# Attention's order in a two-layer trunk: gates and compression directly behind the keys, the values' products and the second queries beside the first group's scores

## The chip, the cores and the metric

The kernel runs on one core of a Trainium2 chip. Its engines are TensorE (PE in the profile; its weight loads are shown apart as PEld), VectorE (DVE), ScalarE (ACT), GpSimd (POOL) and SyncE (SP), which issues the transfers. The metric is device microseconds of one execution, all on this one core. The kernel before took 737.44 us (median of 3 runs: 737.44, 735.28 and 738.83).

## The reference, cut to what matters

x is 256 positions by 1024 features, all in float32. There are two layers: a gated linear recurrence and a ConvFFN, then native sparse attention and a ConvFFN, each behind an RMSNorm with shift, scale and gate from a conditioning vector, and a last RMSNorm. The change is in the attention:

```python
q, k_c, v_c, k_s, v_s, k_w, v_w, gate = jnp.split(h @ w_in, split_at, axis=-1)   # 1024, 6 x 256, 48
gate = jax.nn.sigmoid(gate.astype(jnp.float32)).reshape(B, S, G, HPG, 3)
kc = compress(k_c, cmp_pe[0], cmp_w1[0], cmp_w2[0])      # silu(blocks @ w1) @ w2, 15 blocks of 32 positions
vc = compress(v_c, cmp_pe[1], cmp_w1[1], cmp_w2[1])
...
p_c = jax.nn.softmax(jnp.where(valid_c, s_c, NEG_INF), axis=-1)      # s_*: scaled q.k less slope x distance
...
return gb[..., 0, None] * o_c + gb[..., 1, None] * o_s + gb[..., 2, None] * o_w
...
return o.astype(h.dtype) @ w_out
```

G = 4 groups of keys and values serve HPG = 4 heads of 64 features each. With 256 positions all four blocks of 64 positions are selected and the window of 512 covers everything, so the second and third branch are causal attention over all positions with two sets of keys and values.

## The kernel before, in words

The features lie on the partitions: XT is [128, 8 chunks, 256 positions]. The weights are float32 and stream through the kernel once, in units of 512 KB (128x1024). A unit is loaded by SP (L91) into one of 7 raw buffers, cast by ScalarE to a high part `whi` (L104), and VectorE subtracts that from the unit for the low part `wlo` (L107); there are 5 pairs of split buffers. Each float32 product is done as three products of such parts: high x high (L311), high weight x low activations (L312), low weight x high activations (L313). Loading runs up to 7 units ahead of the unit in use and splitting up to 3 ahead. Some units are rows of the conditioning's weights (`ada`), which VectorE sums in the raw buffer (L239), without TensorE.

TensorE and SP run in the order in which the program is written. The order of VectorE and ScalarE is made by a scheduler, with priorities given in the program (`soon`, `high_priority`); inside the attention loop GpSimd is in written order too. The names of PSUM buffers are "mm" and "aux" with two banks each and "acc" with four, and a bank is given out again when its last reader is done.

The attention part is written in this order (the numbers of functions and lines are those of the listing below):

- the products for the keys and the compressed branch's inputs, on eight accumulators, then the copies KV of the compression's inputs (L882) and the high and low parts KH and KL of the keys (L886 to L888);
- the values' products `some_values` (48 products of 128x512 into two "mm" banks), five of the eight chunks ahead of the compression and three behind it, with a loop of early splits between (NSA_SPLIT);
- the compression `hps` (32 matmuls), its offset `pec` (L912) and Silu (L915);
- the gates `gps` (24 products) and their sigmoid `gsb` (L930);
- the first queries, `gen_q(0)`: two units of weights, 48 products 128x256; the compressed keys and values (`kps`, L962, L964) lie between the first unit and the second. At its end ScalarE scales a head into the high half of the tile `QS` (L953) and VectorE forms its low half (L954), head after head, four heads;
- the gates' transposes (L982), and the first half of the second queries `gen_q(1)`;
- the loop over the four groups. `weave` runs generators side by side, always the one that is furthest behind by a weight in us. The first is `scores`: for each pair of heads (k = 0, 1) three pieces; in a piece each head has two score products into an "acc" bank (L1014, L1015), VectorE adds the distances and takes the least (L1019), ScalarE takes the exponential (L1023), VectorE forms the compressed scores `SC` (L1026). After the last piece of a pair of heads `scale` multiplies the probabilities PR by gate over sum: for the first 128 query positions (t = 0) on VectorE, tiles of 128x128 (L1042), for the others (t = 1) on GpSimd, tiles of 128x256 (L1044). Beside a group's scores stand the next group's queries and, from the second group on, `gen_values` of the group before: transposes of PR (L1092, L1096), their copies `pt` (L1102), the products with the values (L1116, L1119) and the high and low parts AH and AL of the result (L1125, L1129).

```python
sides.append((gen_q(g + 1) if g else queries, SIDE))
...
weave((heads, SCORES[g]), *sides)
```

Of the kernel before, what the change touches and what calls it, by code (L numbers as in the profile page):

```python
# [11 lines left out]
FT = mybir.dt.float32  # L12
FR = mybir.dt.float32r
U32 = mybir.dt.uint32
AF = mybir.ActivationFunctionType
# [4 lines left out]
P = 128  # L20
D = 1024
NC = 8
S = 256
# [16 lines left out]
HG_LATE = 6  # L40
FFN_LATE = 8
NSA_ROWS = (11, 3)
NSA_SPLIT = 2
PRE = 2
HG_WEAVE = (16.4, 15.5)
HG_TURN = 14
# [2 lines left out]
SIDE, VALUES = 5.6, 9.5  # L49
# [4 lines left out]
QBLOCK = 4  # L54
# [112 lines left out]
def one_after_another(*gens):  # L167
    for g in gens:
        yield from g
# [3 lines left out]
def trunk(ctx: ExitStack, tc: tile.TileContext, I, out):  # L173
    nc = tc.nc
# [7 lines left out]
    def bank(tag):  # L182
        return psum.tile([P, 512], FT, name=tag, bufs=4 if tag == "acc" else 2)

    def soon():

        return tc.high_priority(offset=SOON)
# [38 lines left out]
    XH = consts.tile([P, NC, S], FR, name="XH")  # L226
    XL = consts.tile([P, NC, S], FR, name="XL")
# [6 lines left out]
    st = Stream(nc, raws, splits, *LOOK)  # L234
# [24 lines left out]
    flat = lambda a: a.rearrange("p a b -> p (a b)")  # L259
    pairs = lambda a: [flat(a[:, k:k + 2]) for k in range(0, NC, 2)]  # L260
# [31 lines left out]
        return ids[:NC], get  # L292

    u_f = [ffn_units(0, ada_units(0, "g2") + ada_units(1, "1") + ada_units(1, "g1"))]
    ws = chunks(I["nsa_a"]) + pairs(I["nsa_v"]) + [flat(I["nsa_gate"])] + chunks(I["nsa_q"]) + chunks(I["nsa_out"])
    rows = ada_units(1, "2")
    a, b = NSA_ROWS
    ids = mix(ws[:12], rows[:a])
    for r in rows[a:a + b]:
        ada(r)  # L300
    ids += mix(ws[12:21], []) + mix(ws[21:], rows[a + b:])
    u_na, u_nv, u_ng, u_nq, u_no = ids[:8], ids[8:12], ids[12], ids[13:21], ids[21:29]
    u_f.append(ffn_units(1, ada_units(1, "g2")))

    for h in range(4):
# [4 lines left out]
    def mm3(o, wh, wl, xh, xl, start, stop):  # L310
        nc.tensor.matmul(o, wh, xh, start=start, stop=False, skip_group_check=True)  # L311
        nc.tensor.matmul(o, wh, xl, start=False, stop=False, skip_group_check=True)  # L312
        nc.tensor.matmul(o, wl, xh, start=False, stop=stop, skip_group_check=True)  # L313
# [174 lines left out]
    def token_major(ps, c, hi, lo, w):  # L488

        for t in range(2):  # L490
            x = slice(t * P, (t + 1) * P)
            mm3(ps[t], XH[:, c, x], XL[:, c, x], hi[:, w], lo[:, w], c == 0, c == NC - 1)
            yield 0.65
# [232 lines left out]
    def run(g):  # L726
        for _ in g:
            pass
# [165 lines left out]
        keys(g, slice(P, S), s[:, :P])  # L894
        keys(g, slice(272, 528), half(acc, 6 + g // 2)[b:b + 64])

    vps = [bank("mm") for _ in range(2)]

    def some_values(c0, c1):
        for c in range(c0, c1):  # L900
            hi, lo = st.use(u_nv[c // 2])
            run(token_major(vps, c, hi, lo, slice((c % 2) * 512, (c % 2 + 1) * 512)))

    some_values(0, 5)
    while st.done < u_ng + NSA_SPLIT:
        st.split()

    hps = bank("aux")
    for l in range(32):
# [4 lines left out]
    with soon():  # L914
        nc.scalar.activation(hid, hps[:, :60], AF.Silu, bias=pec)  # L915

    some_values(5, NC)

    for t in range(2):
        (nc.scalar.copy, nc.vector.tensor_copy)[t](VT[:, t].rearrange("p g d -> p (g d)"), vps[t])  # L920


    gps = bank("aux")
    hi, lo = st.use(u_ng)
    for c in range(NC):
        w = slice(c * P, (c + 1) * P)
        mm3(gps[:, :S], hi[:, w], lo[:, w], XH[:, c], XL[:, c], c == 0, c == NC - 1)
    gsb = big.tile([48, S], FT, name="gsb")
    with soon():
        nc.scalar.activation(gsb, gps[:48, :S], AF.Sigmoid)  # L930

    QS, PR = {}, {}

    def gen_q(g):


        ps = bank("mm")
        for k in range(2):
            for c in range(NC):
                hi, lo = st.use(u_nq[2 * g + k])  # L940
                w = slice(c * P, (c + 1) * P)
                mm3(ps[:, k * S:(k + 1) * S], hi[:, w], lo[:, w], XH[:, c], XL[:, c], k == 0 and c == 0, c == NC - 1)
                if c % QBLOCK == QBLOCK - 1:
                    yield 0.35 * QBLOCK
        QS[g] = att.tile([P, HPG, S], FR, name="QS")
        rest = []
        with tc.high_priority(offset=QSOON[g]):
            for k in range(2):
                for b in range(2):
                    src = ps[64 * b:64 * b + 64, k * S:(k + 1) * S]  # L950
                    h = 2 * k + b
                    f = -HD ** -0.5 / slopes[HPG * g + h]
                    nc.scalar.activation(QS[g][:64, h], src, AF.Copy, scale=f)  # L953
                    nc.vector.scalar_tensor_tensor(QS[g][64:, h], src, f, QS[g][:64, h].bitcast(FT),  # L954
                                                   op0=OP.mult, op1=OP.subtract)
        yield 0.01
# [29 lines left out]
    for t in range(2):  # L986
        nc.vector.tensor_scalar(gate[:, t, 0::3], gate[:, t, 0::3], rowok[:, t:t + 1], None, op0=OP.mult)

    queries = gen_q(1)
    for _ in range(NC // QBLOCK):  # L990
        next(queries)

    BANKS = [[(P, 400, [(0, 0, P, 0, 0), (1, 144, P, P, 0)], P)],
# [3 lines left out]
    def scores(g, k):  # L999
# [31 lines left out]
        def scale():  # L1031
            r = work.tile([P, 2, 2, 2], FT, name="rsum", bufs=3)
            nc.vector.reciprocal(r, ssum)
            for b in range(2):
                nc.vector.tensor_mul(r[:, b], r[:, b], gate[:, :, 3 * heads[b] + 1:3 * heads[b] + 3])
            for b in range(2):
                for t in range(2):
                    for _, _, parts, _ in BANKS[t]:
                        for br, f, n, o, d in parts:
                            p = PR[g][t][:, 2 * k + b, o:o + n]  # L1040
                            if t == 0:
                                nc.vector.tensor_scalar(p, p, r[:, b, t, br:br + 1], None, op0=OP.mult)  # L1042
                            else:
                                nc.gpsimd.tensor_scalar(p, p, r[:, b, t, br:br + 1], 0.0, op0=OP.mult, op1=OP.add)  # L1044
# [102 lines left out]
    with tc.manual_schedule(engines={ET.Pool}):  # L1147
        st.lazy = True
        for g in range(G):
            heads = one_after_another(*[scores(g, k) for k in range(2)])  # L1150
            sides = []
            if g + 1 < G:
                sides.append((gen_q(g + 1) if g else queries, SIDE))
                if g > 0:
                    sides.append((after(BEHIND[0], gen_values(g - 1)), BEHIND[0] + VALUES))
                for _ in range(HEAD[g]):
                    next(heads)
            else:

                acc_o = [bank("acc") for _ in range(4)]  # L1160
                outs = [out_chunk(acc_o, u_no[j], AH[:, j], AL[:, j], j == 0, 4) for j in range(6)]
                next(heads)
                run(outs[0])
                sides.append((after(BEHIND[1], gen_values(g - 1)), BEHIND[1] + VALUES))
                sides.append((one_after_another(*outs[1:BESIDE]), 2.64 * (BESIDE - 1)))
            weave((heads, SCORES[g]), *sides)
        gate_cols(2)
        weave((gen_values(3), VALUES), (one_after_another(*outs[BESIDE:6]), 2.64 * (6 - BESIDE)))
        st.flush()
        st.lazy = False  # L1170
# [97 lines left out]
```

## Time and profile before

| | |
|---|---|
| time, 3 runs | 737.44 us median (735.28 to 738.83) |
| the profiled execution's own time | 740.72 us |
| its span | 738.9 us |
| granted TensorE clock, mean | 0.976 |
| busy share: PE, DVE, ACT, POOL | 95%, 77%, 52%, 14% |
| HBM over the span | 216 GB/s |

The span goes from the first to the last instruction of the profiled execution. Busy time is that of an engine's instructions; time in which an engine waits is not in it. A row of a timeline gives the start, the duration, engine and line, operation, output and inputs, shapes, and in brackets how long the engine sat idle before it and what ended that. Products run in a pipeline: two neighbours start 0.12 us apart though each takes 0.28. The clock is given as a share of the higher of its two levels, 2.4 GHz; 0.5 is the lower, 1.2 GHz.

### The profile page before, as it was taken

To read this page: it belongs to the slowest core of one execution; us is meant where nothing else is said; L and a number is where in the kernel's file an instruction comes from. 1 tells how busy PE (TensorE), PEld (TensorE's weight loads), DVE (VectorE), ACT (ScalarE), POOL (GpSimd) and SP (SyncE) were. 2 spreads that over 40 slices of the span, in tenths; PEclk is the share of its full clock that TensorE was granted. 3 is DMA by queue.
4 is the path that set the end of the run, shared out by engine and by line. 5 is a ranking of instruction groups with operands and counts; after the bars stand their busy time and mean duration, and the time that the engine had idled before them with its cause. 6 is when DMAs were issued, how large, how long until landed. Compare 5 with 4: busy or idle time off the path is not lost.

```text
span 738.9 us, 14320 instructions
## 1 busy us (share of the span) xinstructions
PE 700.9 (95%) x5532; PEld 665.3 (90%) x5532; DVE 572.4 (77%) x1115; ACT 382.1 (52%) x706; POOL 106.3 (14%) x150
## 2 busy tenths in 40 slices
PE   8999899899999999999999997889999999999996
PEld 7878888788999999999999896767899999999995
DVE  5999999998898777789879778986477866666653
ACT  5337444154655444555444667764355555445544
POOL 2000001012012182101130002222110110100112
PEclk8999999999999999999999998999999999999997
DMA  8898757578488888999939951321237676767601
GB/s 315 295 333 314 254 155 251 167 252 290 166 309 286 273 281 279 282 306 339 328 111 321 342 173 33 112 79 40 83 122 250 218 216 198 216 210 221 206 2 57
DMA packets 48854, 160.45 MB, mean 217 GB/s; under 512 B 9361, under 2 KB 9617, under 8 KB 48786
## 3 DMA queue, kind: packets, MB, share of 16 engines
q1 hardware_dynamic: 48496, 159.02, 65.7%
q8 instruction: 43, 0.70, 0.4%
q10 hardware_dynamic: 290, 0.53, 0.2%
q14 instruction: 25, 0.20, 0.1%
HBM read 158.48 MB, written 1.05 MB: 216 GB/s over the span
## 4 chain that ended last, share of the span: by engine, by line
PE 69%; DVE 15%; DMA 5%; issue 4%; ACT 4%; POOL 2%; POOLq 0%; DVEq 0%; ACTq 0%; SPq 0%
PE mm L311 10%; PE mm L313 10%; PE acc L374 10%; PE mm L312 10%; PE acc L313 6%; PE acc L312 6%; PE acc L311 6%; DVE wlo L107 5%; DMA raw<-ada 4%; DVE raw L239 4%; PE aux L597 2%; DMA raw<-hg_out 2%; POOL sq L347 1%; PE aux L1096 1%; PE mm L1119 1%
## 5 line engine op out<-in xcount | busy, mean ns | idle before, releaser
L107 DVE TENSOR_TENSOR wlo<-raw,whi 128x1024 fp32r<-128x1024 f32 x201 | 247.7, 1238 | 69.5 <-ACT whi L104 69.4
L104 ACT CAST whi<-raw 128x1024 fp32r<-128x1024 f32 x201 | 208.0, 1048 | 147.6 <-PE mm L312 45.9
L311 PE MATMUL mm<-XH,whi 128*128 128x256 f32 x672 | 189.6, 282 | 2.0 <-DVE AL L1129 1.1
L313 PE MATMUL mm<-XH,wlo 128*128 128x256 f32 x672 | 188.6, 281 | 0.4 <-DVE wlo L107 0.4
L312 PE MATMUL mm<-XL,whi 128*128 128x256 f32 x672 | 188.2, 280 | 0.0
L239 DVE SCALAR_TENSOR_TENSOR raw<-raw,cb 128x1024 f32<-128x1024 f32 x96 | 119.0, 1242 | 23.5 <-DMA raw<-ada 23.4
L311 PEld LDWEIGHTS mm<-XH,whi 128*128 128x128 f32 x672 | 127.0, 189 | 3.1 <-DVE ff L792 1.5
L313 PEld LDWEIGHTS mm<-XH,wlo 128*128 128x128 f32 x672 | 127.1, 189 | 0.7 <-DVE wlo L107 0.6
L312 PEld LDWEIGHTS mm<-XL,whi 128*128 128x128 f32 x672 | 127.1, 189 | 0.0
L312 PE MATMUL acc<-fl,whi 128*128 128x256 f32 x352 | 98.6, 280 | 0.3 <-POOL fl L797 0.3
L311 PE MATMUL acc<-fh,whi 128*128 128x256 f32 x352 | 98.5, 280 | 0.0
L313 PE MATMUL acc<-fh,wlo 128*128 128x256 f32 x352 | 98.5, 280 | 0.0
L797 POOL TENSOR_TENSOR fl<-ff,fh 128x256 fp32r<-128x256 f32 x44 | 42.8, 977 | 302.5 <-ACT fh L795 294.9
L312 PEld LDWEIGHTS acc<-fl,whi 128*128 128x128 f32 x352 | 66.2, 188 | 0.5 <-POOL fl L797 0.5
L313 PEld LDWEIGHTS acc<-fh,wlo 128*128 128x128 f32 x352 | 66.2, 188 | 0.0
L311 PEld LDWEIGHTS acc<-fh,whi 128*128 128x128 f32 x352 | 66.1, 188 | 0.0
L790 ACT ACTIVATE cv<-cv 128x256 f32<-128x256 f32 x44 | 18.0, 415 | 46.5 <-DVE cv L789 46.3
L374 PE MATMUL acc<-XH,whi 128*128 128x256 f32 x256 | 37.9, 292 | 3.8 <-ACT XH L393 3.8
L374 PEld LDWEIGHTS acc<-XH,whi 128*128 128x128 f32 x256 | 33.9, 196 | 7.1 <-ACT XH L393 7.0
L393 ACT ACTIVATE XH<-xn,sh_t 128x256 fp32r<-128x256 f32 x32 | 15.2, 503 | 41.6 <-DVE xn L392 41.6
L795 ACT CAST fh<-ff 128x256 fp32r<-128x256 f32 x44 | 17.5, 405 | 35.5 <-DVE ff L792 35.4
L374 PE MATMUL acc<-XL,whi 128*128 128x256 f32 x256 | 35.3, 279 | 0.0
(230 smaller groups left out, 1218.6 us busy)
## 6 DMA issues: line engine op xcount, KB each, us to landing
raw<-ada SPq DMA_DIRECT2D x96, 512.0 KB, 4.8
raw<-up SPq DMA_DIRECT2D x88, 512.0 KB, 4.6
raw<-down SPq DMA_DIRECT2D x44, 512.0 KB, 4.6
raw<-hg_a SPq DMA_DIRECT2D x16, 512.0 KB, 5.2
raw<-hg_b SPq DMA_DIRECT2D x8, 512.0 KB, 5.0
raw<-hg_out SPq DMA_DIRECT2D x8, 512.0 KB, 4.5
raw<-nsa_a SPq DMA_DIRECT2D x8, 512.0 KB, 4.8
raw<-nsa_q SPq DMA_DIRECT2D x8, 512.0 KB, 5.4
```

The costliest lines, as they stand in the source:

```text
L104: self.nc.scalar.copy(hi, t)
L107: low.tensor_sub(lo, t, hi.bitcast(FT))
L239: nc.vector.scalar_tensor_tensor(t, t, 1.0, cb, op0=OP.mult, op1=OP.mult, accum_out=mod[:, n:n + 1])
L311: nc.tensor.matmul(o, wh, xh, start=start, stop=False, skip_group_check=True)
L312: nc.tensor.matmul(o, wh, xl, start=False, stop=False, skip_group_check=True)
L313: nc.tensor.matmul(o, wl, xh, start=False, stop=stop, skip_group_check=True)
L374: nc.tensor.matmul(half(accs, m), a[:, w], x[:, c], start=c == 0 and m % 2 == 0 and n == 0, stop=c == NC - 1 and n == 2, skip_group_check= ...
L393: hi = nc.scalar.activation(XH[:, c], xn, AF.Identity, bias=sh)
L597: nc.tensor.matmul(ps[:, (2 * h + t) * 64:(2 * h + t + 1) * 64], self.KS[:, h, x], q, start=True, stop=True)
L790: nc.scalar.activation(t, t, AF.Silu)
L795: nc.scalar.copy(fh, f)
L797: return nc.gpsimd.tensor_sub(fl, f, fh.bitcast(FT))
```

## The change

Four things change in the attention part. First, the gates' products stand directly behind the keys' and the compression behind the gates'; the loop of early splits goes. Second, the values' products become a generator, `gen_v`, and run together with the second queries, one after the other, beside the first group's scores, with a weight of 10.4 + SIDE = 16.0. No part of the second queries runs ahead of the loop any more. Third, the units are loaded in the order of their new use: keys, gate, two query units, four value units, the other query units. Fourth, of the scalings of the first 128 positions, those of a group's first pair of heads (k = 0) move from VectorE to GpSimd: 2 heads x 2 tiles x 4 groups, 16 of 32.

```diff
-    ws = chunks(I["nsa_a"]) + pairs(I["nsa_v"]) + [flat(I["nsa_gate"])] + chunks(I["nsa_q"]) + chunks(I["nsa_out"])
+    q = chunks(I["nsa_q"])
+    ws = chunks(I["nsa_a"]) + [flat(I["nsa_gate"])] + q[:2] + pairs(I["nsa_v"]) + q[2:] + chunks(I["nsa_out"])
...
-    u_na, u_nv, u_ng, u_nq, u_no = ids[:8], ids[8:12], ids[12], ids[13:21], ids[21:29]
+    u_na, u_ng, u_nq, u_nv, u_no = ids[:8], ids[8], ids[9:11] + ids[15:21], ids[11:15], ids[21:29]
...
-    vps = [bank("mm") for _ in range(2)]
-    def some_values(c0, c1):
-        for c in range(c0, c1):
-            hi, lo = st.use(u_nv[c // 2])
-            run(token_major(vps, c, hi, lo, slice((c % 2) * 512, (c % 2 + 1) * 512)))
-    some_values(0, 5)
-    while st.done < u_ng + NSA_SPLIT:
-        st.split()
+    gps = bank("aux")
+    hi, lo = st.use(u_ng)
+    for c in range(NC):
+        w = slice(c * P, (c + 1) * P)
+        mm3(gps[:, :S], hi[:, w], lo[:, w], XH[:, c], XL[:, c], c == 0, c == NC - 1)
...
     hps = bank("aux")
...
-    some_values(5, NC)
...
+    def gen_v():
+        ps = [bank("mm") for _ in range(2)]
+        for c in range(NC):
+            hi, lo = st.use(u_nv[c // 2])
+            yield from token_major(ps, c, hi, lo, slice((c % 2) * 512, (c % 2 + 1) * 512))
+        for t in range(2):
+            (nc.scalar.copy, nc.vector.tensor_copy)[t](VT[:, t].rearrange("p g d -> p (g d)"), ps[t])
...
-    queries = gen_q(1)
-    for _ in range(NC // QBLOCK):
-        next(queries)
...
-                            if t == 0:
+                            if t == 0 and k == 1:
                                 nc.vector.tensor_scalar(p, p, r[:, b, t, br:br + 1], None, op0=OP.mult)
...
-                sides.append((gen_q(g + 1) if g else queries, SIDE))
+                if g:
+                    sides.append((gen_q(g + 1), SIDE))
+                else:
+                    sides.append((one_after_another(gen_v(), gen_q(1)), 10.4 + SIDE))
```

What TensorE runs at the end of the first queries, before: `mm_4954` is the first queries' bank, `mm_5048` the second queries', `gsb` the gates.

```order
L313 MATMUL mm_4954<-XH_89,wlo_4921 128x256
L982 MATMUL aux_5041<-ident_79,gsb_4952 128x48 x2
L311 MATMUL mm_5048<-XH_89,whi_4924 128x256
L312 MATMUL mm_5048<-XL_90,whi_4924 128x256
L313 MATMUL mm_5048<-XH_89,wlo_4925 128x256
```

And in the changed kernel at the same place: `mm_4854` is the first queries' bank, `QS_4938` their scaled heads, `acc_...` the score banks, `mm_4988` the first of the values' two banks.

```order
L313 MATMUL mm_4854<-XH_89,wlo_4860 128x256
L976 MATMUL aux_4947<-ident_79,gsb_4815 128x48 x2
L1004 MATMUL acc_4960<-KH_1937,QS_4938 128x272
L1005 MATMUL acc_4960<-KL_1938,QS_4938 128x272
L1004 MATMUL acc_4961<-KH_1937,QS_4938 128x272
L1005 MATMUL acc_4961<-KL_1938,QS_4938 128x272
L1004 MATMUL acc_4976<-KH_1937,QS_4938 128x272
L1005 MATMUL acc_4976<-KL_1938,QS_4938 128x272
L1004 MATMUL acc_4977<-KH_1937,QS_4938 128x272
L1005 MATMUL acc_4977<-KL_1938,QS_4938 128x272
L311 MATMUL mm_4988<-whi_4909,XH_89 128x512
L312 MATMUL mm_4988<-wlo_4910,XH_89 128x512
```

The first 24 products of the second queries no longer stand between the first queries' last product and the first score. One product further on, the values' other bank, `mm_4989`, is written for the first time.

What TensorE runs where the second group begins, before: `QS_5032` are the first group's scaled queries, `QS_5194` the second's, `mm_5249` the third queries' bank.

```order
L1014 MATMUL acc_5204<-KH_1937,QS_5032 128x256
L1015 MATMUL acc_5204<-KL_1938,QS_5032 128x256
L1014 MATMUL acc_5217<-KH_1937,QS_5194 128x272
L1015 MATMUL acc_5217<-KL_1938,QS_5194 128x272
L1014 MATMUL acc_5218<-KH_1937,QS_5194 128x272
L1015 MATMUL acc_5218<-KL_1938,QS_5194 128x272
L311 MATMUL mm_5249<-XH_89,whi_5004 128x256
```

And in the changed kernel, where `mm_5133` is the second queries' bank and `QS_5204` their scaled heads.

```order
L313 MATMUL mm_5133<-XH_89,wlo_5056 128x256
L1004 MATMUL acc_5217<-KH_1937,QS_5204 128x272
L1005 MATMUL acc_5217<-KL_1938,QS_5204 128x272
L1004 MATMUL acc_5218<-KH_1937,QS_5204 128x272
L1005 MATMUL acc_5218<-KL_1938,QS_5204 128x272
L311 MATMUL mm_5249<-XH_89,whi_5103 128x256
```

The last products of the second queries stood ahead of twelve score products of the first group and the second group's first; now they stand directly ahead of the second group's first scores, and the first group's scores lie between the products of the values and of the second queries.

ScalarE at the scaling of the second queries, before: `PR...` are exponentials of the first group, `whi_5353` is the cast of a weight unit of the output projection.

```order
L1023 ACTIVATE PR0_5081,ssum_5153<-PR0_5081,nmin_5152 128x128
L953 ACTIVATE QS_5194<-mm_5048 64x256
L1023 ACTIVATE PR0_5081,ssum_5153<-PR0_5081,nmin_5152 128x128 x3
L953 ACTIVATE QS_5194<-mm_5048 64x256
L1023 ACTIVATE PR1_5082,ssum_5153<-PR1_5082,nmin_5152 128x256
L104 CAST whi_5353<-raw_5002 128x1024
```

And in the changed kernel, where `VT` is the copy of the values, `SC0` the exponential of the compressed scores, and `whi_5176`, `whi_5252` and `whi_5353` are casts of weight units.

```order
L926 COPY VT_1939<-mm_4988 128x512
L103 CAST whi_5176<-raw_5014 128x1024
L1044 ACTIVATE SC0_1941<-SC0_1941 128x8x16
L1013 ACTIVATE PR1_4957,ssum_5063<-PR1_4957,nmin_5062 128x256 x2
L103 CAST whi_5252<-raw_5053 128x1024
L103 CAST whi_5353<-raw_5101 128x1024
L947 ACTIVATE QS_5204<-mm_5133 64x256 x2
```

The scaling of the second queries stood among the first group's exponentials, ahead of the cast of `whi_5353`; now it stands behind those exponentials and behind that cast.

## Rows read from the trace of the kernel before

**Rows 1.** The page's first part: busy time, share, instructions of each engine.

```profile
PE 700.9 (95%) x5532; PEld 665.3 (90%) x5532; DVE 572.4 (77%) x1115; ACT 382.1 (52%) x706; POOL 106.3 (14%) x150
```

**Rows 2.** Stretches: length, busy PE, PEld, DVE, ACT, POOL, clock, DMA share, GB/s.

```profile
437.00:443.00 6.00, 5.88 (x48) 5.54 (x46) 5.04 (x25) 5.79 (x16) 0.00 (x0) 1.00 0.35 111
443.00:450.00 7.00, 2.26 (x10) 1.64 (x10) 6.62 (x35) 6.90 (x26) 1.93 (x4) 0.87 0.26 77
448.00:449.00 1.00, 0.00 (x0) 0.00 (x0) 0.95 (x5) 1.00 (x3) 0.96 (x3) 0.56 0.00 0
450.00:455.00 5.00, 5.00 (x25) 5.00 (x24) 3.68 (x26) 2.41 (x13) 2.02 (x4) 0.51 0.00 0
455.00:512.00 57.00, 50.01 (x367) 40.47 (x366) 48.27 (x202) 36.99 (x121) 14.05 (x24) 0.97 0.26 75
```

**Rows 3.** TensorE's waits, 380 to 510 us: us in total, times, longest.

```profile
PE acc L1014 <- DVE SC L1026: 4.0, 3, 1.7
...
PE acc L1014 <- DVE rsum L1033: 0.7, 1, 0.7
```

**Rows 4.** TensorE's timeline from 444 us, start and duration first.

```profile
444.69 0.36 PE L1014 MATMUL acc<-KH,QS 128*128 128x256 f32 x1 [1.59 <-DVE SC L1026]
444.89 0.28 PE L1015 MATMUL acc<-KL,QS 128*128 128x256 f32 x1
```

**Rows 5.** TensorE's timeline around the first scores.

```profile
433.85 0.28 PE L313 MATMUL mm<-XH,wlo 128*128 128x256 f32 x1
...
437.24 0.29 PE L1014 MATMUL acc<-KH,QS 128*128 128x272 f32 x1
...
437.77 0.39 PE L1014 MATMUL acc<-KH,QS 128*128 128x272 f32 x1
```

**Rows 6.** ScalarE's timeline around the first scores.

```profile
434.09 1.05 ACT L104 CAST whi<-raw 128x1024 fp32r<-128x1024 f32 x1 [1.16 <-PE mm L312]
...
436.88 0.38 ACT L953 ACTIVATE QS<-mm 64x256 fp32r<-64x256 f32 x1 [1.08 <-DVE QS L954]
437.36 1.05 ACT L104 CAST whi<-raw 128x1024 fp32r<-128x1024 f32 x1
```

**Rows 7.** VectorE's timeline around the first scores.

```profile
435.17 1.23 DVE L107 TENSOR_TENSOR wlo<-raw,whi 128x1024 fp32r<-128x1024 f32 x1
436.43 0.42 DVE L954 SCALAR_TENSOR_TENSOR QS<-mm,QS 64x256 fp32r<-64x256 f32 x1
...
441.44 0.43 DVE L954 SCALAR_TENSOR_TENSOR QS<-mm,QS 64x256 fp32r<-64x256 f32 x1 [0.53 <-ACT QS L953]
```

**Rows 8.** Lines of scalings: ns least/median/most, first and last start.

```profile
L1042 DVE TENSOR_SCALAR PR<-PR,rsum x32: 273/282/544, 446.9 to 510.2; 128x128 f32<-128x128 f32 x32
L1044 POOL TENSOR_SCALAR PR<-PR,rsum x32: 477/484/1505, 447.0 to 510.2; 128x256 f32<-128x256 f32 x32
L862 POOL TENSOR_SCALAR tabc<-later x16: 217/218/1184, 270.1 to 277.8; 128x32 f32<-128x32 f32 x16
```

**Rows 9.** TensorE's waits, 456 to 512 us.

```profile
PE mm L1119 <- DVE AL L1129: 1.8, 2, 0.9
PE aux L1014 <- DVE pt L1102: 1.2, 1, 1.2
PE aux L1096 <- DVE nmin L1019: 1.1, 1, 1.1
PE mm L311 <- DVE AL L1129: 1.1, 1, 1.1
```

**Rows 10.** Timelines of VectorE and GpSimd from 462 us.

```profile
462.25 1.22 DVE L107 TENSOR_TENSOR wlo<-raw,whi 128x1024 fp32r<-128x1024 f32 x1
...
462.43 2.88 POOL L1044 TENSOR_SCALAR PR<-PR,rsum 128x256 f32<-128x256 f32 x4 [9.08 <-DVE rsum L1035]
```

**Rows 11.** ScalarE's timeline, a table load.

```profile
428.51 1.28 ACT L930 ACT_TABLE_LOAD   x1
```

**Rows 12.** SP's timeline: transfers issued for the query weights.

```profile
406.48 12.88 SPq L91 DMA_DIRECT2D raw<-nsa_q  x8
```

More of the change, by code (lines that the diff above doesn't have):

```diff
@@ L42 @@
 NSA_ROWS = (11, 3)
-NSA_SPLIT = 2
 PRE = 2
@@ L895, in trunk @@
         keys(g, slice(272, 528), half(acc, 6 + g // 2)[b:b + 64])
-    vps = [bank("mm") for _ in range(2)]
-    def some_values(c0, c1):
-        for c in range(c0, c1):
-            hi, lo = st.use(u_nv[c // 2])
-            run(token_major(vps, c, hi, lo, slice((c % 2) * 512, (c % 2 + 1) * 512)))
-    some_values(0, 5)
-    while st.done < u_ng + NSA_SPLIT:
-        st.split()
+    gps = bank("aux")
[3 more added lines that the diff above has]
+        mm3(gps[:, :S], hi[:, w], lo[:, w], XH[:, c], XL[:, c], c == 0, c == NC - 1)
+    gsb = big.tile([48, S], FT, name="gsb")
+    with soon():
+        nc.scalar.activation(gsb, gps[:48, :S], AF.Sigmoid)
     hps = bank("aux")
@@ L915, in trunk @@
         nc.scalar.activation(hid, hps[:, :60], AF.Silu, bias=pec)
-    some_values(5, NC)
[L919 to L930, printed above, removed]
-    QS, PR = {}, {}
+    QS, PR = {}, {}
+    def gen_v():
[5 more added lines that the diff above has]
+            (nc.scalar.copy, nc.vector.tensor_copy)[t](VT[:, t].rearrange("p g d -> p (g d)"), ps[t])
     def gen_q(g):
```

## The prediction

> **What bounds the kernel now.** I read the page's first part, then the busy time by stretch, then who is waited for in the attention part, then the instructions there one by one. TensorE is busy 700.9 of the 738.9 us [rows 1], so a change of order can win only in the few places where TensorE stands still or runs slowly. The stretches show one such place [rows 2]. From 437 to 443 us TensorE is busy for 5.88 of 6.00 us, 48 products at 0.1225 us each. From 443 to 450 it is busy for 2.26 of 7.00 us while ScalarE is busy for 6.90 and VectorE for 6.62: there the last piece of the first group's scores and the first piece of the second group's stand alone, with no other product beside them. The waits say the same: 4.0 + 0.7 us of waiting for VectorE, each time because a score bank has not been read yet [rows 3]. Within that stretch the granted clock drops (0.56 from 448 to 449, with no product at all), and from 450 to 455 TensorE is full but at 0.51, the lower of its two levels: 25 products in 5.00 us, 0.20 us each instead of 0.1225 [rows 2]. That costs 25 x 0.08 = 2.0 us, with the edges some 2.3. From 455 to 512 TensorE is idle for 57.00 - 50.01 = 7.0 us and VectorE busy for 85%.
>
> So the attention part loses about 4.7 + 2.3 + 7.0 us in all, and nothing that the change does can win more than these 14.
>
> **The change part by part.** Terms are differences against the profiled execution (740.72 us, span 738.9); that lies 3.3 us above the median of the runs, and I put the sum on the median, 737.44. The products are the same before and after, so TensorE's work cancels.
>
> *The stretch from 443 to 450 goes.* The first group's score pieces now have the values' 48 products and the second queries' 48 beside them, so a bank is read while products run. The idle 4.74 us go [rows 2]. A pair of score products that stands alone takes from 444.69 to 444.89 + 0.28, 0.5 us [rows 4]; run closely behind others it takes 2 x 0.1225. Four such pairs: -1.0 us. Together -5.7.
>
> *The first score loses its cover.* Before, the last product of the first queries starts at 433.85 and the first score at 437.24; 24 products of the second queries lie in between, and the second head's score follows at 437.77 [rows 5]. The scores need the queries as scaled tiles, one after the other on two engines: ScalarE casts the next weight unit (434.09, 1.05 us) and then scales head 0; VectorE subtracts for that weight unit (435.17, 1.23 us), then makes head 0's low part (436.43, 0.42); only then does ScalarE go on to head 1 (436.88, after 1.08 us of waiting for VectorE) [rows 6, 7]. From 433.97 to 437.77 this chain is 3.8 us long. In the changed order only the gate's two transposes (0.25) and head 0's score pair (0.25) lie in it, and the cast and the subtraction of a weight unit still stand in front of head 0. Before, 0.3 us of the chain were uncovered. So 3.8 - 0.5 - 0.3 = +3.0. Bounds: with neither cast nor subtraction in it the chain is two times 0.38 + 0.42, hence 1.6 - 0.8 = +0.8; with one more subtraction +4.2. I take +3.0, since the queue in front is the one that the rows show.
>
> *The values' second bank.* It is the bank that held the first queries, free when the last head's low part has been made. Before, that ends at 441.44 + 0.43 [rows 7], 4.1 us after the second score. One cast of 1.05 us (437.36) that stood in between no longer does [rows 6]; the table load for the exponential stays. TensorE's own work until it wants the bank is three score pairs and three values' products, some 1.45 us. 4.1 - 1.05 - 1.45 = +1.6, bounds 0 (these are all done by then) and 2.65 (a cast takes that place).
>
> *The second group's first score.* It now stands directly behind the last product of the second queries, where before the second queries were finished while the first group's scores still ran. The chain is that of the first score again, and ahead of it ScalarE casts two weight units, the second of which needs a buffer that TensorE frees with that last product. 3.8 less head 0's score pair: +3.5, bounds 1.4 (no cast, no subtraction) and 5.0 (both casts and a subtraction late).
>
> *The clock.* Before, it falls once, after a stretch of 6.2 us with 2 us of work. The new stretch around the first scores is about as empty (some 6 us with under 2 us of work in it), so I expect one fall again: 0, bounds -2.3 (none) and +2.3 (a second one at the second group).
>
> *Less work on VectorE.* Sixteen of its 32 scalings of 128x128 (0.282 us each [rows 8]) go to GpSimd: 4.5 us. From 455 to 512 TensorE's waits that VectorE ends are 1.8 + 1.2 + 1.1 + 1.1 us [rows 9], with some smaller ones 5.4; a faster VectorE can remove between none and all of that, and I take half, -2.7. What GpSimd pays: its scaling of 128x256 takes 0.484 us and one of 128x32 0.218 [rows 8], in between a 128x128 by columns some 0.33, 5.3 us in all; GpSimd is busy for 14.05 of these 57.00 us [rows 2], so that is hidden. The cover is thinner where a group's first scaled half is transposed soon after.
>
> One rule speaks against this edit. While GpSimd scaled four tiles from 462.43, VectorE subtracted a weight unit from 462.25; the four took 2.88 us, 1.5 times four of 0.484, and the subtraction 1.22, as elsewhere [rows 7, 8, 10]. Here GpSimd came second and paid. The Trainium skill ("SBUF — State Buffer", section "SBUF: two separate sides") says that a VectorE operation with two SBUF inputs and a GpSimd operation that reads SBUF exclude each other, and that the one that starts later waits for the whole of the other. The trace agrees for this order of starting; the other order, in which VectorE would pay for each added scaling, no row here shows.
>
> *What is hidden.* The gates in front of the compression cost nothing by themselves: 24 products (2.9 us) stand where 30 wider ones stood, and cover the two copies that the compression reads. One more table load for ScalarE (1.28 us [rows 11]) lies behind the first half of the first queries (2.9 us); without that cover it costs 1.3. The values' weights are asked for behind two query units instead of in front of the gates; SP's queue had all eight query units out by 406.48 + 12.88 us [rows 12], and the values' products now stand behind gates, compression and first queries, so their weights have landed long before. The removed loop of early splits costs nothing since casts now follow the usual look-ahead.
>
> Sum: -4.7 - 1.0 + 3.0 + 1.6 + 3.5 + 0 - 2.7 = -0.3 us, so 737.1.
>
> **The rivals.** The measurement of this kernel can tell about 0.5% (3.7 us) from no change, so what follows is set against 733.75 and 741.1.
>
> *A, VectorE was the bound of the whole stretch.* Then pulling scores forward to where VectorE had time, beside the values' products, is worth more than half of its later waits: all 5.4 us, and the clock has no empty stretch long enough to fall, -2.3. 8.1 of new waits - 5.7 - 2.3 - 5.4 = -5.3, 732.1. For it: VectorE is busy for 95% of 443 to 450 and 85% of 455 to 512 [rows 2]. Against it: the waits after 456 also have ScalarE's copies behind them, and the chain through the queries' scaling is made of waits from one engine to the other, which no free time shortens.
>
> *B, two holes in place of one (slower).* The two new chains, at the first score and at the second group's, each leave TensorE with under 1 us of work in over 3. If the clock falls behind both, one more slow stretch costs +2.3, and if the later waits are bound by ScalarE, the relief is only -0.5: 8.1 - 5.7 + 2.3 - 0.5 = +4.2, 741.6. [...] For it: the clock did fall in a stretch like that [rows 2]. Against it: products at full pace stand right before and behind.
>
> *C, GpSimd holds up VectorE (slower).* If each added scaling starts first and VectorE stands behind it, VectorE gains nothing, and of the 5.3 us of scalings half lies in places where TensorE waits for VectorE: 2.4 + 2.65 = +5.05, 742.5. By the skill's rule above this is what would happen. Against it: the trace shows GpSimd, not VectorE, paying.
>
> That the order doesn't change as meant I exclude: the rows of the order show it.
>
> **How the numbers follow.** Forecast 0.47 (its own range 733.75 to 741.1), A 0.31, B 0.18, C 0.04. Faster by over 0.5%: A, 0.31. Within 0.5%: 0.47. Slower: B and C, 0.22. The range must reach into A on the one side, whose floor is below its own 732.1 if one of the new waits turns out at its lower bound, and to C on the other: 730.5 to 743.0.
>
> **What would show it.** Right: no stretch of 5 us with TensorE under half busy between the groups, but two gaps of 3 to 4 us, directly ahead of the second head's first score and ahead of the second group's first score, with VectorE's low part of the queries as what is waited for; a gap of 1 to 2 us ahead of the second product of the values; one stretch of slow clock; fewer waits for VectorE's rows of the value part, about 2.7 us less. GpSimd's scalings of 128x128 at some 0.33 us, and VectorE's subtractions still at 1.2. Wrong: if the gap at the first score is under 1.5 us the chain was not what held the score (towards A); if the waits from the second group on are as long as before, half of the relief was too much (towards B); if subtractions of VectorE take clearly over 1.23 us beside scalings, C.

## The result, and the profile after

The changed kernel took 741.64 us (median of 7 runs, 738.54 to 742.76), the kernel before 736.41 (7 runs, 733.72 to 738.83): a ratio of 1.0061 with a 95% interval of 1.0036 to 1.0087, some 4.5 us slower. 737.1 had been forecast, with no change that can be measured; the time is that of rival B (741.6). The profiled execution of the changed kernel has a span of 739.9 us. From the first product behind the keys to the start of the last group of value products it takes 530.82 - 402.78 = 128.0 us, the kernel before 528.92 - 404.96 = 124.0: 4.1 us more in the attention part. The rest of the two profiled executions, with the same work in it, differs by 3.2 us the other way, so one profile is not the mean of a kernel's executions. The attention part of before and then of the changed kernel:

```profile
404.96:528.92 123.96, 112.11 (x798) 96.05 (x796) 94.31 (x337) 79.37 (x227) 17.99 (x32) 0.96 0.41 130
```

```profile
402.78:530.82 128.04, 113.44 (x798) 96.54 (x797) 91.01 (x319) 81.15 (x227) 27.00 (x48) 0.95 0.39 125
```

TensorE stands still for 14.60 us of it instead of 11.85, 2.75 us more, and the same products keep it busy for 1.33 us longer.

The first part of the page and the busy time by stretch of the changed kernel answer to [rows 1, 2]; the columns are the same, and two stretches of before stand behind them.

```profile
PE 699.6 (95%) x5532; PEld 663.3 (90%) x5532; DVE 569.6 (77%) x1099; ACT 384.3 (52%) x707; POOL 116.7 (16%) x166
```

```profile
420.00:425.00 5.00, 1.94 (x14) 1.46 (x13) 4.18 (x11) 3.19 (x8) 0.00 (x0) 1.00 0.80 270
425.00:430.00 5.00, 4.05 (x13) 2.88 (x13) 3.96 (x20) 4.27 (x14) 0.00 (x0) 0.55 0.20 79
450.00:455.00 5.00, 2.21 (x10) 2.02 (x11) 4.01 (x16) 2.14 (x9) 1.61 (x1) 0.78 0.86 287
455.00:460.00 5.00, 5.00 (x40) 5.00 (x40) 2.98 (x15) 3.44 (x11) 0.00 (x0) 0.88 0.05 20
...
456.00:512.00 56.00, 49.78 (x367) 41.27 (x366) 42.08 (x182) 37.36 (x121) 16.65 (x34) 0.97 0.20 58
500.00:505.00 5.00, 4.42 (x25) 3.96 (x24) 2.04 (x14) 3.00 (x10) 2.17 (x6) 0.66 0.25 93
```

```profile
456.00:512.00 56.00, 49.01 (x358) 39.47 (x357) 48.18 (x202) 36.59 (x121) 14.05 (x24) 0.97 0.27 76
505.00:510.00 5.00, 4.92 (x27) 4.15 (x28) 3.25 (x15) 2.63 (x9) 1.28 (x3) 0.66 0.21 84
```

The empty stretch of before (443 to 450) is gone. In its place there are two, from 420 to 425 and from 448 to 452, and behind each of them the granted clock is at the lower level for a while. From 456 to 512 VectorE has some 6 us less to do than before, and TensorE is idle for 6.2 us where it was 7.0. Near the end of the attention part the clock falls once more in both kernels (0.66), so before it falls twice in this part and not once, and in the changed kernel three times.

TensorE's waits from 380 to 510 us (in total, times, longest) answer to [rows 3, 9].

```profile
PE acc L1004 <- DVE QS L948: 7.4, 4, 3.4
PE mm L1109 <- DVE AL L1119: 1.8, 2, 0.9
PE aux L1086 <- POOL PR L1034: 1.2, 1, 1.2
PE mm L311 <- DVE AL L1119: 1.1, 1, 1.1
PE mm L311 <- DVE QS L948: 0.9, 1, 0.9
PE aux L1004 <- DVE pt L1092: 0.8, 1, 0.8
```

The score bank that had not been read (4.0 + 0.7) is out of the list. 7.4 + 0.9 us of waiting for the low part of the scaled queries stand in its place. One wait of 1.2 us has changed its releaser: the transposes waited for VectorE's reduction (1.1 us before) and now wait for a scaling on GpSimd.

TensorE's timeline shows the four waits, the slow products and their normal pace; it answers to [rows 4, 5].

```profile
420.49 0.28 PE L313 MATMUL mm<-XH,wlo 128*128 128x256 f32 x1
423.54 0.39 PE L1004 MATMUL acc<-KH,QS 128*128 128x272 f32 x1 [2.52 <-DVE QS L948]
424.60 0.39 PE L1004 MATMUL acc<-KH,QS 128*128 128x272 f32 x1 [0.54 <-DVE QS L948]
427.88 0.77 PE L311 MATMUL mm<-whi,XH 128*128 128x512 f32 x1 [0.95 <-DVE QS L948]
430.58 0.63 PE L311 MATMUL mm<-whi,XH 128*128 128x512 f32 x1
431.01 0.63 PE L312 MATMUL mm<-wlo,XH 128*128 128x512 f32 x1
433.23 0.40 PE L311 MATMUL mm<-whi,XH 128*128 128x512 f32 x1
433.46 0.40 PE L312 MATMUL mm<-wlo,XH 128*128 128x512 f32 x1
448.14 0.28 PE L313 MATMUL mm<-XH,wlo 128*128 128x256 f32 x1
451.85 0.39 PE L1004 MATMUL acc<-KH,QS 128*128 128x272 f32 x1 [3.43 <-DVE QS L948]
453.31 0.57 PE L1004 MATMUL acc<-KH,QS 128*128 128x272 f32 x1 [0.94 <-DVE QS L948]
```

From the last product of the first queries (420.49 + 0.12) to the second head's score it is 4.0 us. At the second group it is 3.6 us to the first head's score (448.26 to 451.85) and 5.1 us to the second head's (453.31). Thirteen values' products behind the first gap start 0.43 us apart instead of 0.23, 2.5 us lost; eleven of the third queries behind the second gap 0.21 instead of 0.12, 1.0 us.

VectorE at the second group, the queue ahead of the low part for which TensorE waits (it answers to [rows 7]):

```profile
447.64 1.23 DVE L106 TENSOR_TENSOR wlo<-raw,whi 128x1024 fp32r<-128x1024 f32 x1
448.79 1.41 DVE L238 SCALAR_TENSOR_TENSOR raw<-raw,cb 128x1024 f32<-128x1024 f32 x1
450.13 1.21 DVE L106 TENSOR_TENSOR wlo<-raw,whi 128x1024 fp32r<-128x1024 f32 x1
451.38 0.42 DVE L948 SCALAR_TENSOR_TENSOR QS<-mm,QS 64x256 fp32r<-64x256 f32 x1
```

Two subtractions and a row of the conditioning stand in front of the low part. ScalarE's timeline at the same place, which answers to [rows 6]:

```profile
448.38 1.04 ACT L103 CAST whi<-raw 128x1024 fp32r<-128x1024 f32 x1 [1.49 <-issue]
449.33 0.37 ACT L947 ACTIVATE QS<-mm 64x256 fp32r<-64x256 f32 x1
```

The high part was ready at 449.70, 1.7 us before VectorE came to the low part. GpSimd's timeline there, which answers to [rows 10]:

```profile
446.61 5.00 POOL L1034 TENSOR_SCALAR PR<-PR,rsum 128x256 f32<-128x256 f32 x4 [6.75 <-DVE rsum L1025]
```

Four scalings of 128x256 take 5.00 us beside those VectorE rows, four times 0.484 being their usual time [rows 8], and VectorE's subtractions 1.21 and 1.23 as always; the row of the conditioning took 1.41, where its median is 1.22.

### The profile page after: what moved, and what is told of

The parts are those of the page before. It is cut to its first block, busy times and chain, and to the rows that moved or that the text cites. A ratio compares the mean times of both kernels' runs of the same rounds, so it can differ in the third digit from the quotient of the medians.

```text
span 739.9 us, 14322 instructions
## 1 busy us (share of the span) xinstructions
PE 699.6 (95%) x5532; PEld 663.3 (90%) x5532; DVE 569.6 (77%) x1099; ACT 384.3 (52%) x707; POOL 116.7 (16%) x166
## 4 chain that ended last, share of the span: by engine, by line
PE 75%; DVE 15%; issue 4%; ACT 3%; POOL 2%; DMA 1%; POOLq 0%; DVEq 0%; ACTq 0%; SPq 0%
PE mm L311 11%; PE mm L313 11%; PE mm L312 11%; PE acc L374 10%; PE acc L313 7%; PE acc L311 7%; PE acc L312 7%; DVE wlo L106 5%; DVE raw L238 4%; PE aux L597 2%; PE mm L1109 1%; PE aux L1086 1%; POOL sq L347 1%; PE aux L910 1%; DMA raw<-hg_out 1%
## 5 line engine op out<-in xcount | busy, mean ns | idle before, releaser
L1034 POOL TENSOR_SCALAR PR<-PR,rsum 128x256 f32<-128x256 f32 (+1 forms) x48 | 27.0, 582 | 108.8 <-PE mm L313 58.2
```

## The experiments

Theory O: the new order costs, because the queries' chain (cast, high part, low part, over two engines) now lies open twice and the clock falls behind both gaps. Rival S: the scalings on GpSimd cost. All ratios below are to the kernel before, run on the same chip at the same time.

**The two halves of the change apart.** The kernel before with the scalings alone:

```diff
-                            if t == 0:
+                            if t == 0 and k == 1:
```

> The kernel before with one edit: the sixteen scalings of 128x128 of the first pairs of heads go from VectorE to GpSimd; the order stays. Theory O (the new order costs: the query chain of casts, scaling and low part is uncovered twice and the clock falls twice): this alone is worth little, -1.5 to 0.5 us against before, ratio 0.998 to 1.001. Theory S (the scalings on GpSimd cost, because the two engines exclude each other): +3 to +5 us, ratio 1.004 to 1.007, and VectorE's subtractions beside them take clearly over 1.23 us.

Measured: 0.9939 (0.9910 to 0.9967), 4.5 us faster. And the changed kernel without them, its order alone:

```diff
-                            if t == 0 and k == 1:
+                            if t == 0:
```

> The changed kernel with all 32 scalings of 128x128 back on VectorE, so the new order alone. Theory O: +4 to +6 us against before, ratio 1.005 to 1.009, with the same 7 to 8 us of waits at the two query chains and two stretches of slow clock. Theory S: within 1 us of before.

Measured: 1.0068 (1.0043 to 1.0094), with 7.4 us of waits for the low parts of the queries as in the changed kernel. S has fallen: the order alone makes it all. But O had the scalings wrong too: alone they win 4.5 us (2.4 to 6.6), on top of the new order 0.5 (1.0061 against 1.0068, less than the intervals tell). Where the first kernel's gain lies, its waits (380 to 540 us) and stretches show:

```profile
PE acc L1014 <- DVE SC L1026: 2.3, 2, 1.6
...
PE aux L1096 <- POOL PR L1044: 1.2, 1, 1.2
...
PE acc L1014 <- DVE rsum L1033: 0.7, 1, 0.7
```

```profile
440.00:445.00 5.00, 2.09 (x14) 1.51 (x12) 4.72 (x23) 4.93 (x22) 0.00 (x0) 1.00 0.35 105
445.00:450.00 5.00, 4.89 (x26) 4.79 (x27) 4.11 (x29) 4.97 (x20) 3.59 (x9) 0.66 0.00 2
450.00:455.00 5.00, 5.00 (x44) 4.43 (x42) 4.10 (x26) 4.03 (x14) 1.73 (x4) 1.00 0.00 0
```

With the first four scalings off VectorE, one of three waits for a score bank is gone (4.0 to 2.3 us; one of 0.6 for a low part is new) and the slow clock is over by 450, where it lasted to 455. The scalings stood in front of the reductions that set the empty stretch; in the changed order that stretch doesn't exist. Counted from the first product behind the keys, this execution is 2.8 us ahead of the one of before at the second group's third piece. Another 1.8 us come behind the fourth group's first score, where it has no second fall of the clock (1.00 from 456 to 512); e3's profile, of another order, has none there either, so that part need not be the scalings' doing. The wait for GpSimd in place of VectorE's reduction, of the same size, is here too.

**The clock, in the changed kernel.** Extra products of XH with itself fill the two gaps:

```diff
+    def fill(n):
+        ps = bank("acc")
+        for _ in range(n):
+            nc.tensor.matmul(ps[:, :S], XH[:, 0, :P], XH[:, 0], start=True, stop=True)
...
+                if g < 2:
+                    fill((21, 28)[g])
```

> The changed kernel with 21 extra products of 128x256 into an unused score bank ahead of the first group's scores and 28 ahead of the second group's, whose results nobody reads: they lie in the two gaps, so the waits stay and the clock should not fall. If the slow clock is what made the change slower by more than the waits: -2.5 to -4 us against the changed kernel (13 products of 128x512 at 0.43 instead of 0.23 us, 11 of 128x256 at 0.21 instead of 0.12), so 0 to +2 against before. If the clock costs nothing: as the changed kernel, +4 to +6.

Measured: 1.0006 (0.9981 to 1.0031), 4.1 us faster than the changed kernel (1.4 to 6.7 by the two intervals) and level with before. The waits are only filled, not shortened, and that for the values' second bank grew from 0.95 to 1.46 us: the slow products ahead of it had been hidden by it. Its stretches behind the two gaps show the clock at 1.00:

```profile
425.00:430.00 5.00, 3.38 (x16) 2.62 (x17) 4.45 (x22) 4.67 (x15) 0.00 (x0) 1.00 0.23 91
450.00:455.00 5.00, 4.58 (x36) 4.16 (x35) 4.12 (x22) 3.82 (x15) 0.12 (x1) 1.00 0.67 230
```

So the slow products behind the two gaps cost about what the rows say (3.5 us). The profiled attention part says the same, 124.0 us (403.36 to 527.40) instead of 128.0. It isn't yet the difference to the kernel before, which has a slow stretch of its own.

**The clock, in the kernel before.** The same for its empty stretch, with a free "aux" bank:

```diff
+    FILL = {(0, 1, 1, 272): (13, 6), (1, 0, 0, P): (6, 14)}
...
+                    if n:
+                        fill(extra, n[b])
```

> The kernel before with 13, 6, 6 and 14 extra products of 128x256 into a free bank ahead of the four score pairs that stand alone between 443 and 450 us; nobody reads them, and each set is about as long as the wait it stands in. The waits stay, the clock should not fall there. If the slow clock behind that stretch costs what the rows show (24 products at 0.21 instead of 0.12 us and two score pairs, 2.3 to 2.8 us): ratio 0.996 to 0.997. With 4.1 us for the same in the changed kernel that leaves 1.3 to 1.8 us of the change's cost to the clock. If the clock's fall there costs nothing: 0.999 to 1.001; if the two orders lose alike to it: 0.994 to 0.995.

Measured: 0.9995 (0.9974 to 1.0016), a gain of 0.4 us (-1.2 to 1.9). The expectation of 0.996 to 0.997 was missed. The clock did stay up, and the time did not follow. First the stretches of this kernel, then the one of before that answers to the last of them:

```profile
443.00:450.00 7.00, 6.93 (x55) 6.58 (x55) 6.84 (x41) 6.51 (x27) 3.66 (x8) 1.00 0.05 19
450.00:455.00 5.00, 5.00 (x42) 4.12 (x40) 4.53 (x24) 4.98 (x19) 0.30 (x1) 1.00 0.02 5
455.00:460.00 5.00, 3.32 (x26) 2.72 (x26) 4.94 (x12) 1.12 (x4) 3.98 (x4) 1.00 0.70 201
```

```profile
455.00:460.00 5.00, 5.00 (x43) 4.33 (x42) 3.53 (x20) 4.37 (x15) 0.00 (x0) 1.00 0.01 2
```

The attention part of this profiled execution, and the wait that is longer in it than in the kernel before (0.9 us there [rows 9]):

```profile
401.88:522.97 121.09, 114.11 (x838) 98.35 (x836) 95.16 (x337) 80.46 (x227) 18.90 (x32) 0.99 0.42 136
457.42 0.65 PE L1129 MATMUL mm<-pt,VT 128*64 128x256 f32 x4 [1.49 <-DVE AL L1139]
```

TensorE passes 450 to 455 at full pace and then stands still for 1.7 us, with VectorE busy for 4.94 of 5 us. But most of what the pace won stays. From the second group's second head to that group's third piece the profile of before takes 6.20 us (449.28 to 455.48), this one 3.65 (446.23 to 449.88): 2.55 us less, as the rows had said. At the third group's first score 2.2 of them are left, and the whole attention part takes 121.1 us instead of 124.0. So in these two executions the slow stretch was hidden behind VectorE only in a small part, and twelve executions against sixteen show no such gain. Their mean granted clocks lie 0.003 apart (0.984 and 0.981), those of the two profiled ones 0.007 (0.983 and 0.976), so the profiled pair differs by more than the kernels do. What the fall is worth in the order of before stays open, between 0.4 and 2.9 us.

In the changed order nothing is taken back: with its gaps filled the third group's first score comes 3.9 us earlier, and the attention part ends 4.0 us earlier.

**The gaps.** The second queries' first half ahead of the loop again, their rest next, the values' products last:

```diff
-                    sides.append((one_after_another(gen_v(), gen_q(1)), 10.4 + SIDE))
+                    sides.append((one_after_another(queries, gen_v()), 10.4 + SIDE / 2))
```

> The changed kernel with the first half of the second queries ahead of the loop again, their rest next and the values' products behind them (beside the first group's scores; units loaded in that order). Theory O: both gaps go (first score covered by 24 products, second group's queries ready long before), no fall of the clock there: -6 to -9 us against before (4.7 of waits, 1.0 of lone pairs, 2.3 of slow clock), ratio 0.988 to 0.992. Theory S: +3 to +5 as the changed kernel, since the scalings are on GpSimd here too. If the values' late end makes a new wait at the third queries' bank: -4 to -6.

Measured: 1.0006 (0.9983 to 1.0028); -6 to -9 us was missed. Both gaps had only moved. Its timeline:

```profile
426.81 0.40 PE L1008 MATMUL acc<-KH,QS 128*128 128x272 f32 x1 [2.49 <-DVE QS L948]
437.70 0.47 PE L311 MATMUL mm<-whi,XH 128*128 128x512 f32 x1 [4.35 <-DVE QS L948]
```

The second head's low part now stands behind the cast and subtraction of a unit that waits for the end of the 24 products, and the values' second bank is that of the second queries, which their last low part frees. So in the next kernel the values take the "aux" banks:

```diff
-        ps = [bank("mm") for _ in range(2)]
+        ps = [bank("aux") for _ in range(2)]
```

> The kernel with the second queries first (e3_queries_first), and the values' products in the two banks named aux in place of the two named mm, so that they no longer wait for the low part of the second queries (4.35 us there in one wait). Theory: the place of the lost time is the queries' chain of scaling, wherever TensorE meets its end; taking the meeting away gives -4 to -6 us against e3_queries_first, ratio to before 0.992 to 0.995 with the wait of 2.5 us at the second head's first score left. Rival: VectorE and ScalarE are simply behind, and the wait comes back at the next score bank: within 1.5 us of e3_queries_first, ratio 0.998 to 1.002.

Measured: 0.9901 (0.9877 to 0.9925), 7.7 us faster than with the values in "mm", where 4 to 6 had been expected. The wait of 4.35 us is gone, that of 2.5 at the second head is left, no other has come up, and the clock is at 1.00 from 404 to 460, where the kernel with the values in "mm" has 0.82 to 0.84 from 425 to 445. The rival (behind in any case) has fallen.

**The priority of the chain.**

```diff
-QSOON = (150, 150, 25, 25)
+QSOON = (600, 600, 25, 25)
```

> The changed kernel with a higher priority for the scaling of the first two groups' queries (QSOON 600 in place of 150). In the order VectorE's subtraction of a weight unit then stands behind the first queries' low parts; at the second group nothing changes, two subtractions and a row of the conditioning stay ahead of the low part. Chain theory: the first gap shrinks by the subtraction, 1.2 us, perhaps with some of the slow clock behind it: -1 to -3 us against the changed kernel, ratio to before 1.002 to 1.005; the second gap stays at 3.4 us. Rival (the gap is set by ScalarE's cast of the unit, which stays ahead): within 0.5 us of the changed kernel, ratio 1.005 to 1.007.

Measured: 1.0055 (1.0033 to 1.0076), 0.4 us below the changed kernel, which doesn't tell the two apart; -1 to -3 us was not reached. The timeline shows what became of the first gap:

```profile
423.83 0.39 PE L1004 MATMUL acc<-KH,QS 128*128 128x272 f32 x1 [1.61 <-DVE QS L948]
425.16 0.39 PE L1004 MATMUL acc<-KH,QS 128*128 128x272 f32 x1 [0.81 <-DVE QS L948]
428.44 0.47 PE L311 MATMUL mm<-whi,XH 128*128 128x512 f32 x1 [1.56 <-DVE QS L948]
450.41 0.43 PE L1004 MATMUL acc<-KH,QS 128*128 128x272 f32 x1 [3.40 <-DVE QS L948]
```

The first gap shrank from 3.1 to 2.4 us. The last low part came 0.6 us earlier, but TensorE was at the values' bank 1.3 us earlier, with a shorter gap and three products at full pace ahead of it, so the wait there grew from 0.9 to 1.6. In this profile the clock is at 1.00 behind the first gap, and the second group's first score comes 2.7 us earlier than in that of the changed kernel; behind the second gap the clock is low for longer, and 1.3 us are lost again. The times of twelve executions show still less. With both edits in the changed order:

> The changed kernel with the higher priority of e6_queries_urgent and the values' banks of e5_values_in_aux, in the changed order. In e6 the first gap shrank by 0.6 us and the wait for the values' second bank, which hangs on the last low part, grew by 0.6; without that bank the gain should stay: the wait of 1.6 us goes, -1.5 to -2.5 us against the changed kernel, ratio to before 1.002 to 1.004. Rival (the wait returns at the score banks behind): within 0.5 us of e6_queries_urgent, ratio 1.005 to 1.007.

Measured: 0.9998 (0.9975 to 1.0021), 4.6 us faster than the changed kernel, more than the 1.5 to 2.5 expected. The clock after the first gap stayed at 1.00 in its profile (as in e6's); after the second it fell. How much of the rest is the clock and how much the spread of one chip against another, these runs do not tell.

Both edits with the queries first:

> e5_values_in_aux with the higher priority of e6_queries_urgent: ScalarE's scaling of the second head no longer stands behind a cast that waits for TensorE's last product of the second queries' first half, nor VectorE's behind its subtraction. Chain theory: the wait of 2.5 us at the second head's first score goes as well: -7 to -9 us against before, ratio 0.988 to 0.991, the fastest so far. Rival (behind in any case): as e5_values_in_aux.

Measured: 0.9887 (0.9861 to 0.9914), 8.3 us faster than before. Against the same order without the priority that is 1.0 us, less than the intervals tell; the profiled attention part is 2.6 us shorter. The wait at the second head is 0.6 us:

```profile
PE mm L1113 <- DVE AL L1123: 1.8, 2, 0.9
PE aux L1090 <- POOL PR L1038: 1.2, 1, 1.2
...
PE acc L1008 <- DVE QS L948: 0.6, 1, 0.6
```

The same with the scalings on VectorE again:

> e7_aux_and_urgent with all 32 scalings of 128x128 on VectorE again. If the scalings' move is worth something only where VectorE is late (in the order of before, 4.5 us; in the changed order, which waits for a chain, about 1): with the gaps closed VectorE is full beside the first group's scores, so it should cost 2 to 4 us, ratio to before 0.991 to 0.995. Rival (the worth comes from the value part of the later groups, the same in every order): it would have shown in the changed order too; then 0.5 to 1.5 us, ratio 0.989 to 0.991.

Measured: 0.9887 (0.9853 to 0.9922), the same. 2 to 4 us had been expected, and no cost was measured, though the two intervals leave some 3 us either way. The profiled attention part is 1.2 us longer, 1.1 of it TensorE standing still, which would be the rival's size. So how little the scalings are worth with the chain covered isn't shown.

**The second gap alone.** The changed kernel with the second queries ahead of the values beside the first group's scores, and the values in "aux":

```diff
-                    sides.append((one_after_another(gen_v(), gen_q(1)), 10.4 + SIDE))
+                    sides.append((one_after_another(gen_q(1), gen_v()), 10.4 + SIDE))
```

> The changed kernel with the second queries beside the first group's scores first and the values' products behind them, the values in the two aux banks; nothing of the second queries runs ahead of the loop. So the first gap (3.1 us) stays, and the second group's gap (4.4 us), the wait for the values' second bank (0.95 us) and the second fall of the clock (about 1.3 us) go. Chain theory: -6 to -7 us against the changed kernel, ratio to before 0.996 to 0.999, between the changed kernel and e5_values_in_aux. Rival (the fall of the clock after the first gap carries most): -1 to -3 us, ratio 1.002 to 1.005.

Measured: 0.9940 (0.9915 to 0.9964), 8.9 us faster than the changed kernel and more than the 6 to 7 expected. The first gap is there as before (2.52 + 0.54 us), with slow clock behind it; the second gap, the wait for the bank and the second slow stretch are gone. From here to e5_values_in_aux it is 2.9 us. That is not the whole worth of the first gap, since e5 still waits 2.5 us at its second head: in the profiled attention parts TensorE stands still for 1.0 us less there (8.46 against 9.44), and the same products take 1.6 us less.

## Why the prediction was wrong

*What bounds the kernel now*: right in the main. The empty stretch went away as said, and its 4.7 us of waits with it. "Before, it falls once" was misread: the mean of 0.97 from 455 to 512 [rows 2] holds a second fall, at 505 to 510. The changed kernel has it too, so the sum is not touched by it.

*The first score loses its cover*, +3.0; *the values' second bank*, +1.6; *the second group's first score*, +3.5, together 8.1: measured 2.52 + 0.54 - 0.3, 0.95 and 3.43 + 0.94, together 8.1. The places were right. That the sum is right to a tenth is luck: the first gap was 0.2 us and the bank wait 0.65 us shorter than said, and the second group's gap 0.9 longer, since a row of the conditioning stood in VectorE's queue as well.

*The clock*, "I expect one fall again: 0": this step failed. The clock fell behind both gaps, and keeping it up there gave 4.1 us, 4.0 in the profiled attention part. Against that stands the one fall of before, at 2.3 in the prediction. The profiled executions bear that price out (2.2 to 2.9) and make the term +1.1 to +1.8; the times give 0.4 and make it +3.7. Which of them holds is open; by both, the second fall is what the term lacked.

*Less work on VectorE*, -2.7: failed as well. VectorE did some 6 us less from 456 to 512, and TensorE's idle time there fell by 0.8. The longest waits after 456 have the length of before (1.8, 1.1, and 1.2 instead of 1.1, which changed from VectorE to GpSimd); they look like chains (high part, low part, bank; transposes, copy, product), which no run here tested by itself. The scalings are worth 0.5 us in the changed order and 4.5 in the order of before, where four of them stood ahead of the reductions of the empty stretch. The prediction looked for their worth in the later waits; a good part of it lay in the stretch that the other half of the change removed.

*Four lone pairs*, -1.0: about half, an estimate, since the pairs behind the gaps are alone too (424.95 - 424.60 = 0.35 us).

With these, -4.7 - 0.5 + 8.1 - 0.8 = 2.1, and with the clock 3.2 to 3.9 by the profiles, against 4.1 in the profiled attention part, or 5.8 by the times; 4.5 was measured (interval 2.7 to 6.4), which fits either. In the profiled attention part the sum missed by 4.4 us. Of these 2.1 are waits (2.75 us more of standing still, 0.7 forecast), nearly all of it the -2.7; 2.3 are the products' pace (1.33 us slower, 1.0 faster forecast), the second fall and half of the lone pairs.

Rival B named mechanism and time: two holes in place of one, and a second fall of the clock. That its 741.6 is the measured median to a tenth is luck, for the interval spans 3.7 us. Its second reason, later waits bound by ScalarE, isn't what the rows show. A's premise (VectorE was the bound of the stretch) fits the order of before, where a wait of 1.7 us went with four scalings, but not what A drew from it. C has fallen: of four scalings beside VectorE's work GpSimd paid 5.00 us instead of 1.94, VectorE's subtractions nothing, its row of the conditioning 0.2. The Trainium skill's rule ("SBUF — State Buffer", section "SBUF: two separate sides") agrees with a GpSimd that waits while VectorE's operations with two inputs run; a case in which VectorE waited for a whole scaling (0.48 us) didn't turn up.

## What to carry to other kernels

When a block of products is moved, look at what it covered where it stood: here 24 products over a chain between two other engines, without which 2.8 us of the chain lay open. A result that TensorE needs should be finished a whole block before the block that uses it (queries first, values last, in banks that those queries don't hold: 7.3 us faster than before, where the change lost 4.5), and a bank's last reader counts as part of such a chain. Count the falls of the clock in the new order one by one, each with the products behind it, and price a freed engine by the waits it ends in the stretch where it lies. One profile shows one execution: where the profile and the times of a dozen executions differ by some 2 us, as in the kernel before with its stretch filled, neither settles the price alone.

## What the runs showed of the hardware

Filling two gaps of 3 and 4 us with products that nobody reads kept the granted clock at 1.00 behind them (0.55 and 0.78 without) and gave 4.1 us. The same in the empty stretch of before kept the clock up as well; its times gave 0.4 us, its profiled attention part 2.9. The clock does not fall in the same places in each execution: from 375 to 385 us, ahead of all changed products, it fell in the profiles of before (0.67) and of the changed kernel (0.77), and stayed at 1.00 in those of the same two kernels with their gaps filled. GpSimd's scaling of 128x128 has a mean of 0.43 us in the changed kernel and a least of 0.37, against the estimate of 0.33 from its neighbours.
